# A third column block of w_down by the seven-product scheme, in a one-core decoder layer

## The chip, the cores and the metric

The kernel runs on one core of a Trainium2 chip. The metric is the device time of one execution in microseconds. TensorE (PE in the profile) multiplies, VectorE (DVE) and ScalarE (ACT) work on tiles element by element, GpSimd (POOL) and SyncE (SP) issue transfers between HBM and the on-chip memory SBUF. TensorE writes into eight accumulator banks (PSUM), each 128 partitions by 512 numbers of fp32.

## The reference

One decoder layer over 256 tokens plus 16 meta tokens, model width 2048, inner width 8192, everything in fp32. What matters here is its last part:

```python
u = rms_norm(h, g_pre_mlp[l])
f = jnp.square(jax.nn.relu(u @ w_up[l])) @ w_down[l]     # (256, 8192) @ (8192, 2048)
h = h + rms_norm(f, g_post_mlp[l])
```

Ahead of it stand a combined projection `u @ w_in`, a pooling branch, a convolution branch, and `m @ w_o`.

## The kernel before

**Precision.** Each fp32 matrix is split into a high part (a cast to fp32r on ScalarE) and a low part (the rest, a subtraction on VectorE), and a product is formed as high x high, high x low and low x high. A loaded block of weights is 1 MB, 128 partitions by 2048 numbers. It lies in a raw room; its two parts lie in rooms `hi0..hi2` and `lo0..lo2`, used in turn. So the parts of one product can only be written once the product three places earlier has been multiplied.

**Pieces.** The MLP runs over the inner width in NP = 8 pieces of PF = 1024. In each piece, `u @ w_up` makes 1024 columns (eight products U, named U h pair half: `U0a0` is half h = 0, pair a, first 1024 rows of w_up). Two products finish a pair of up tiles, which is summed out of the banks, scaled, put through relu and squared, and split into parts (`up_pair`, `relu_squared`). Then comes `f += s @ w_down` for that piece, with two token tiles t and two inner halves h of 512. The 2048 columns of w_down form four blocks n of 512 columns.

**Seven products.** Blocks 0 and 1 together are a 2 x 2 problem: token tiles by inner halves on one side, inner halves by column blocks on the other. The kernel solves it by Winograd's form of Strassen's scheme, with seven products P1 to P7 in place of eight. Each P multiplies one form of the activations (`A1`, `A2`: the plain tiles; `S1` to `S4`: sums and differences of them, held in `forms`) by one block of weights or a sum of blocks: `B11`, `B12`, `B21`, `B22`. The sums are made in the raw rooms by VectorE (`SUM_FOR`, 2.29 us planned each), for P5, P6, P7 and P4. `give` adds the finished bank to the result F in SBUF. Blocks 2 and 3 are multiplied plainly: X1 to X4, each one (h, n) for both token tiles, 24 matmuls of 512 columns, into the banks `x00, x01` (block 2) and `x10, x11` (block 3), which stay open over all pieces.

**Order.** A `Plan` collects the work with planned costs (2.72 us for 12 matmuls, 2.29 for a low part, 1.91 for a high part, a load 3.2 on SP plus 2.0 until it lands), the tiles read and written, and orders each engine by start times and due times that it works out from these. TensorE (PE) and SP keep the order in which the work was added; VectorE, ScalarE and GpSimd may be reordered when the program is built. Each engine then runs its own list in order. TensorE's order in a piece is in the strings `PIECE` and `NEXT`; a `+` marks a product of the next piece:

```python
PIECE = "U1a0 U1a1 P1 X1 U1b0 U1b1 X3"
NEXT = "U0a0+ P5 X2 P6 X4 P7 U0a1+ P3 U0b0+ P2 U0b1+ P4"
```

`weights(m)` adds sums and splits up to two products ahead. There are five raw rooms in the MLP (tiles a, c and three raw_m). `loads` hands a free room to the next block in `to_load`, and its transfer waits on SP until the room's last reader is through; SP issues in order. The bank `b` takes P5, P3 and P2 (`BANK`), bank `a` the others.

**Elsewhere.** In the w_o stage two blocks are added to a raw room by the transfer itself: `add_second` (line 1020) issues an adding transfer from GpSimd, planned with 1.0 + 9.0 us. Ahead of everything, the normed input u lies in one tile of 16 feature tiles.

Of the kernel before, what the change touches and what calls it, by code (L numbers as in the profile page):

```python
# [8 lines left out]
F32 = mybir.dt.float32  # L9
# [5 lines left out]
P = 128  # L15
# [6 lines left out]
class Plan:  # L22
# [29 lines left out]
    def order(self):  # L52
        n = len(self.work)
        after = [[] for _ in range(n)]
        for i, (_, _, _, before, _) in enumerate(self.work):
            for b in before:
                after[b].append(i)
        due, t = [float("inf")] * n, 0.0
        for i, (engine, cost, _, _, _) in enumerate(self.work):
            if engine == "PE":  # L60
                due[i] = t
                t += cost
        for i in reversed(range(n)):
            _, cost, _, _, late = self.work[i]
            for a in after[i]:
                due[i] = min(due[i], due[a] - cost - late - self.HOP)
        missing = [len(w[3]) for w in self.work]
        free_at = [0.0] * n
        clock = {w[0]: 0.0 for w in self.work}
        queue = {e: [i for i in range(n) if self.work[i][0] == e] for e in clock}  # L70
        start = [0.0] * n

        def begin(i):
            return max(clock[self.work[i][0]], free_at[i])
        for _ in range(n):
# [12 lines left out]
            queue[e].remove(best)  # L88
            for a in after[best]:
                free_at[a] = max(free_at[a], clock[e] + late + self.HOP)  # L90
                missing[a] -= 1
        self.start = start
        return sorted(range(n), key=lambda i: (start[i], i))

    def emit(self):
        for i in self.order():
            self.work[i][2]()


@with_exitstack  # L100
def hybrid_block(ctx: ExitStack, tc: tile.TileContext, ins: dict, out: bass.AP):
# [6 lines left out]
    NT = T // P  # L108
    KD = D // P
    w_in = ins["w_in"][0]  # L110
    w_grp = ins["w_pool_grp"][0]
# [271 lines left out]

    u = big.tile([P, KD, 2, -(-L // (4 * LINE)) * 4 * LINE], F32R, tag="um", name="u")[:, :, :, :L]

    def meta_tokens():
# [8 lines left out]
        nc.vector.tensor_mul(mg, pt, g[:, :, None].broadcast_to([P, KD, M]))  # L395
        nc.vector.tensor_copy(u[:, :, 0, :M], mg)
        return mg

    mg = meta_tokens()

    def low_of_meta():
        nc.vector.tensor_sub(u[:, :, 1, :M], mg, f32(u[:, :, 0, :M]))

# [173 lines left out]
    x_tile(0)  # L577
    low_of_meta()
    row(0)
# [5 lines left out]
    for k in range(KD):  # L585
# [3 lines left out]
        if k in (0, 2):  # L589
            for kx in (k + 2, k + 3):  # L590
                x_tile(kx)
                row(kx)
        elif k % 2 == 0 and k + 3 < KD:
            x_pair(k + 2)
        elif k + 3 < KD and k > 1:
            row(k + 3)
            row(k + 4)
        squares = {6: (0, 0), 8: (1, 0)}
        if k in squares:
# [753 lines left out]
    products = [s for s in steps if s[0] != "R"]  # L1353


    RAW_OF = {"P1": "B11", "P5": "B11", "P6": "B11", "P4": "B11", "P3": "B22", "P7": "B12",
              "P2": "B21"}
# [17 lines left out]
    for m_, (s, i) in enumerate(products):  # L1375
        if m_ >= len(opened):
            if s in SUM_FOR:
                uses.append((m_, "sum", [(r, i) for r in SUM_FOR[s]]))
            uses.append((m_, "split", [raw_of(s, i)]))
    last_use = {}  # L1380
    to_load = []
# [21 lines left out]
    for m_, (hi_, lo_, _, _) in enumerate(opened):  # L1403
        split_at[m_] = {"hi": hi_, "lo": lo_}

    def weights(m_):

        while uses and uses[0][0] <= m_:
            done = len(last_use_order) - len(uses)
            _, what, raws_ = uses.pop(0)  # L1410
            rooms = [room_at[r] for r in raws_]
            names = [f"raw{r}" for r in rooms]
            if what == "sum":
                a_, b_ = (room_of[r][:, :CK * CW] for r in rooms)
                plan.add("DVE", 2.29, lambda: nc.vector.tensor_add(a_, a_, b_),
                         reads=names, writes=names[:1])
            else:
                box = split_at[m_] = {}
                raw = room_of[rooms[0]][:, :CK * CW]
                n, q = first_n + m_, (first_n + m_) % 3  # L1420
                up = products[m_][0][0] == "U"
                rows = HALF[0] if up else CK

                def high():
                    box["flat"] = part_tile("hi", n, up)
                    nc.scalar.copy(box["flat"], raw)  # L1426
                    box["hi"] = box["flat"].rearrange("p (k c) -> p k c", k=rows)

                def low():
                    lo = part_tile("lo", n, up)  # L1430
                    nc.vector.tensor_sub(lo, raw, f32(box["flat"]))  # L1431
                    box["lo"] = lo.rearrange("p (k c) -> p k c", k=rows)
                plan.add("ACT", 1.91, high, reads=names, writes=(f"hi{q}",))
                plan.add("DVE", 2.29, low, reads=names + [f"hi{q}"], writes=(f"lo{q}",))
            for r in raws_:
# [64 lines left out]
    def relu_squared(h, pr, i, s_name, box):  # L1500
        ks = slice(2 * pr, 2 * pr + 2)
        G = forms[h]

# [13 lines left out]
        def q_(f):  # L1517
            return Q[:, f, ks, :]
        A = f"A{h}{pr}"
        plan.add("ACT", 0.75, square, reads=(s_name,), writes=(s_name,))  # L1520
# [5 lines left out]
        elif i < NP - 1:  # L1526
# [5 lines left out]
            plan.add("DVE", 0.42, lambda: nc.vector.tensor_add(q_(S4Q), a_(A1), q_(S2Q)),  # L1532
                     reads=(s_name, f"q3{pr}"), writes=(f"q4{pr}",))

        def dst(part):
# [25 lines left out]
    def up_done(h, pr, i, accs, acc_names):  # L1561
# [3 lines left out]
        else:  # L1565
            up_pair(h, pr, i, accs, acc_names, "s",
                    lambda: Q[:, SQ].rearrange("p k t -> p (k t)"))

# [19 lines left out]

    GIVES = {"P1": (0, 0, 1, True), "P2": (0, 0, 1, False), "P3": (0, 1, 1, False),
             "P4": (1, 0, 1, True), "P5": (1, 1, 1, True), "P6": (0, 1, -1, True),  # L1590
             "P7": (1, 1, -1, False)}


    def give(s, i):
        t, n, sign, first_ = GIVES[s]
        bank, dst, name = banks[BANK[s]], F[:, t, n, :], f"F{2 * t + n}"

        def f():
            if i == 0 and first_:
                nc.vector.tensor_scalar_mul(dst, bank, float(sign))  # L1600
# [21 lines left out]
    def product_plain(m_, s, i):  # L1622
        h, n = AT[s]
        for t, f in ((0, A1), (1, A2)):
            name = f"x{n - 2}{t}"
            plan.add("PE", 2.72, lambda t=t, f=f, name=name: down(
                banks[name], split_at[m_], h, f, i == 0 and h == 0,
                h == 1 and i == NP - 1 - (n == 3)),
# [17 lines left out]
    def product_block(m_, s, i):  # L1646
        h, f = FORM[s]
        plan.add("PE", 2.72, lambda: down(banks[BANK[s]], split_at[m_], h, f, s in OPENS, True),
                 reads=half_names(m_) + act_names(h, f), writes=(BANK[s],))
        give(s, i)  # L1650


# [27 lines left out]
    for s, i in steps:  # L1680
        if s == "R":
# [10 lines left out]
        {"U": product_up, "X": product_plain, "P": product_block, "Y": product_last}[s[0]](m_, s, i)  # L1692
        m_ += 1
# [40 lines left out]

    col_halves = [slice(h * HALF_CW, (h + 1) * HALF_CW) for h in range(2)]
    for e, cs in enumerate(col_halves):
# [88 lines left out]
```

## Time and profile before

| | us |
|---|---|
| median of 3 runs | 1206.31 (1206.03 to 1206.81) |
| profiled execution, its own time | 1206.4 |
| its span, first to last instruction | 1204.3 |
| TensorE busy | 1194.9 (99%) |
| VectorE busy | 974.5 (81%) |
| ScalarE busy | 624.3 (52%) |
| MLP pieces, from about 554 to the end | 84.4 each |

The profile records one execution. Matmuls overlap in their pipeline, so the time from one start to the next is what a matmul takes from the span, not the duration listed. In the lists of groups, the numbers behind the bar are the total busy time, the mean of one in nanoseconds, and the idle time of the engine just ahead of them with what ended it. The time to landing of a transfer is counted from its issue. In the view by stretches, each row gives the length, then for PE, PEld (weight loads), DVE, ACT and POOL the busy time and the number of instructions, then the granted clock of TensorE, the busy share of the DMA engines and GB/s.

### The profile page before, as it was taken

What the parts mean: (1) busy time and instruction counts of PE and PEld (TensorE: products, weight loads), DVE (VectorE), ACT (ScalarE), POOL (GpSimd) and SP (SyncE); (2) the same over time, 40 slices, a digit from 0 to 9 for tenths busy, and PEclk for the clock granted to TensorE, in tenths of its full rate; (3) what the DMA queues carried; (4) which work ended last, traced back from release to release, by engine and by line L of the source; (5) the groups of instructions that cost most, each with busy time, mean ns of one, the idle gap of its engine ahead of it and who ended that gap; (6) DMA issues with size and microseconds to landing.
All of it is one profiled execution on the core that took longest, in us unless ns stands there. A gap on an engine that the chain in (4) does not pass through costs nothing.

```text
span 1204.3 us, 15707 instructions
## 1 busy us (share of the span) xinstructions
PE 1194.9 (99%) x6442; PEld 1037.6 (86%) x6442; DVE 974.5 (81%) x1055; ACT 624.3 (52%) x633; POOL 8.8 (1%) x23
## 2 busy tenths in 40 slices
PE   9999999999999999999999999999999999999997
PEld 9999988888888888898888888888888888888886
DVE  6899978999676778688988878788878778788756
ACT  6533344443584455665555564564554555554543
POOL 1000000000000000000000000000000000000000
PEclk9999999999999999999999999999999999999999
DMA  9655555656558588546475665674764764755841
GB/s 290 210 177 183 187 189 185 200 186 199 183 167 285 169 267 262 169 168 217 146 239 175 192 227 163 196 250 139 244 199 157 261 198 151 245 175 173 276 146 70
DMA packets 162646, 238.27 MB, mean 198 GB/s; under 512 B 4145, under 2 KB 92401, under 8 KB 162064
## 3 DMA queue, kind: packets, MB, share of 16 engines
q1 hardware_dynamic: 160000, 230.64, 58.6%
q0 software_dynamic: 1680, 5.40, 1.7%
q10 hardware_dynamic: 896, 1.25, 0.3%
q8 instruction: 50, 0.82, 0.3%
q14 instruction: 20, 0.16, 0.0%
HBM read 235.17 MB, written 2.10 MB: 197 GB/s over the span
## 4 chain that ended last, share of the span: by engine, by line
PE 99%; DVE 1%; ACT 0%; DVEq 0%; ACTq 0%; issue 0%
PE bank_u L463 18%; PE acc_gate L746 14%; PE acc_up L1580 14%; PE bank_u L469 9%; PE bank_a L1580 7%; PE o_c L1084 6%; PE bank_b L1580 5%; PE acc_z L458 4%; PE acc_co L746 4%; PE acc_po L746 4%; PE acc_v L458 3%; PE acc_g L458 3%; PE acc_vg L458 2%; PE acc_up L463 1%; PE bank_u L1580 1%; PE o_a L1084 1%
## 5 line engine op out<-in xcount | busy, mean ns | idle before, releaser
L463 PE MATMUL bank_u<-m,hi 128*128 128x512 f32 x960 | 329.9, 390 | 0.0
L469 PE MATMUL bank_u<-m,lo 128*128 128x256 f32 x960 | 265.5, 277 | 0.0
L259 ACT CAST hi<-raw 128x2048 fp32r<-128x2048 f32 (+2 forms) x94 | 151.2, 1619 | 190.5 <-PE acc_gate L746 67.7
L1431 DVE TENSOR_TENSOR lo<-raw_m,hi 128x2048 fp32r<-128x2048 f32 x85 | 194.5, 2290 | 59.6 <-ACT hi L1426 59.5
L1426 ACT CAST hi<-raw_m 128x2048 fp32r<-128x2048 f32 x85 | 162.4, 1911 | 138.1 <-PE bank_u L463 76.8
L463 PEld LDWEIGHTS bank_u<-m,hi 128*128 128x128 f32 x960 | 180.2, 188 | 38.0
L262 DVE TENSOR_TENSOR lo<-raw,hi 128x2048 fp32r<-128x2048 f32 (+2 forms) x94 | 180.1, 1925 | 39.5 <-ACT hi L259 39.2
L469 PEld LDWEIGHTS bank_u<-m,lo 128*128 128x128 f32 x960 | 180.3, 188 | 1.6
L746 PE MATMUL acc_gate<-hi,u 128*128 128x512 f32 x512 | 158.4, 390 | 0.0
L1580 PE MATMUL acc_up<-hi,forms 128*128 128x512 f32 x496 | 157.5, 389 | 0.0
L524 DVE SCALAR_TENSOR_TENSOR c<-a,taps,c 128x256 f32<-128x256 f32 x240 | 115.7, 484 | 6.8
L746 PEld LDWEIGHTS acc_gate<-hi,u 128*128 128x128 f32 x512 | 96.1, 188 | 19.9
L1580 PEld LDWEIGHTS acc_up<-hi,forms 128*128 128x128 f32 x496 | 93.1, 188 | 19.5
L746 PE MATMUL acc_gate<-lo,u 128*128 128x512 f32 x256 | 99.6, 389 | 0.0
L1580 PE MATMUL acc_up<-lo,forms 128*128 128x512 f32 x248 | 96.6, 389 | 0.0
L1431 DVE TENSOR_TENSOR lo<-raw_c,hi 128x2048 fp32r<-128x2048 f32 x29 | 66.4, 2290 | 21.2 <-ACT hi L1426 21.2
L1580 PE MATMUL bank_a<-hi,forms 128*128 128x512 f32 (+1 forms) x256 | 82.0, 383 | 0.0
L1426 ACT CAST hi<-raw_c 128x2048 fp32r<-128x2048 f32 x29 | 55.3, 1908 | 51.0 <-PE bank_u L463 27.9
L1431 DVE TENSOR_TENSOR lo<-raw_a,hi 128x2048 fp32r<-128x2048 f32 x29 | 66.4, 2290 | 17.5 <-ACT hi L1426 17.5
L1426 ACT CAST hi<-raw_a 128x2048 fp32r<-128x2048 f32 x29 | 55.4, 1910 | 42.4 <-PE bank_u L463 19.4
L1084 PE MATMUL o_c<-hi,m 128*128 128x512 f32 x208 | 65.6, 390 | 0.0
L1580 PE MATMUL bank_b<-hi,forms 128*128 128x512 f32 (+1 forms) x200 | 63.7, 382 | 0.0
(327 smaller groups left out, 1850.8 us busy)
## 6 DMA issues: line engine op xcount, KB each, us to landing
raw<-in_w_in_dram SPq DMA_DIRECT2D x52, 1024.0 KB, 5.2
raw_m<-in_w_down_dram SPq DMA_DIRECT2D x37, 1024.0 KB, 5.2
raw_m<-in_w_up_dram SPq DMA_DIRECT2D x33, 1024.0 KB, 6.4
raw_c<-in_w_down_dram SPq DMA_DIRECT2D x14, 1024.0 KB, 5.1
raw_a<-in_w_up_dram SPq DMA_DIRECT2D x13, 1024.0 KB, 6.0
raw_a<-in_w_down_dram SPq DMA_DIRECT2D x13, 1024.0 KB, 5.3
raw_c<-in_w_up_dram SPq DMA_DIRECT2D x12, 1024.0 KB, 5.8
raw_o<-in_w_o_dram SPq DMA_DIRECT2D x10, 1024.0 KB, 7.4
```

The costliest lines, as they stand in the source:

```text
L259: nc.scalar.copy(hi[:, sl, cs], raw[:, sl, cs])
L262: nc.vector.tensor_sub(lo[:, sl, cs], raw[:, sl, cs], f32(hi[:, sl, cs]))
L458: nc.tensor.matmul(acc, w[:, k[0], cs], act[:, k[1], a, off:], start=first and n == 0, stop=last and n == 2)
L463: nc.tensor.matmul(acc.rearrange("p (a t) -> p a t", a=2)[:, :, ts], hi[:, k[0], cs], act[:, k[1], :, off + ts.start:off + ts.stop], start ...
L469: nc.tensor.matmul(acc[:, :T], lo[:, k[0], cs], act[:, k[1], 0, off:], start=False, stop=stop, skip_group_check=True)
L524: nc.vector.scalar_tensor_tensor(c, conv["a"][:, q, i:i + T], taps[:, q, i:i + 1], c, op0=ALU.mult, op1=ALU.add)
L746: nc.tensor.matmul(acc, act(kk)[:, a_, ts_], w_[:, k, :], start=kk == 0 and n == 0, stop=kk == nk - 1 and n == 2)
L1084: nc.tensor.matmul(acc, form(k, a_), box[w_][:, k, :], start=start and k == 0 and n == 0, stop=stop and k == CK - 1 and n == 2, skip_group ...
L1426: nc.scalar.copy(box["flat"], raw)
L1431: nc.vector.tensor_sub(lo, raw, f32(box["flat"]))
L1580: nc.tensor.matmul(acc, forms[h][:, f, k, a_, :], box[w_][:, k, cs], start=start and k == 0 and n == 0, stop=stop and k == KH - 1 and n == ...
```

## The change

Block 2 of w_down is now computed by the same seven-product scheme, its two column halves of 256 taking the place of the two column blocks. X1 and X2 stay the names of its two loaded blocks (h = 0 and 1). Where a piece multiplied X1 and X2 (two 512-column products each), it now multiplies E1 to E5, seven products of 12 matmuls with 256 columns. E1 has P1 and P5 of the scheme side by side in bank `b`, E2 has P2 and P3 in `x00`, E3 puts P6 onto P1 in bank `b`, E4 puts P4 into `x01`, E5 puts P7 onto P1 + P6. After E1, E3 and E5 ScalarE copies the bank out (`save_e`) and VectorE adds or subtracts it into `x00` and `x01` (`add_e`). The sums of weights T1 to T4 are made on half-width columns in the raw rooms (`sum_e`). E4 needs only half a block split, and E5 reads E3's parts again. The last piece keeps X1 and X2.

The sums for P5 (B11 + B12) and P7 (B12 + B22) are no longer made by VectorE: GpSimd issues an adding transfer of the second block onto the room that holds the first (`BRINGS`). For P5 this follows P1's split; for P7 it stands six products ahead, and B12 is loaded for it.

The order of products in a piece is new, the sums of the up tiles' pairs lie in four rooms in place of one (three of them in the tile `pairs`), and the parts of the next piece's activations are written after the last product that reads the old ones (`deferred`). The tile u is two tiles, of 13 and 3 feature tiles, so that `pairs` can take the place of the second one. The bank x01 is set to zero ahead of the pieces. The planner no longer counts a hop between two operations of one engine.

```diff
-                free_at[a] = max(free_at[a], clock[e] + late + self.HOP)
+                hop = self.HOP if self.work[a][0] != e else 0.0
+                free_at[a] = max(free_at[a], clock[e] + late + hop)
...
+    BRING_AHEAD = 6
...
-    u = big.tile([P, KD, 2, -(-L // (4 * LINE)) * 4 * LINE], F32R, tag="um", name="u")[:, :, :, :L]
+    u = Tiles([big.tile([P, n, 2, -(-L // (4 * LINE)) * 4 * LINE], F32R, tag=tag,
+                        name=f"u_{tag}")[:, :, :, :L] for tag, n in (("um", KM), ("ux", KD - KM))], KM)
...
+    pairs_room = big.tile([P, 3, 2 * T], F32, tag="ux", name="pairs")
...
-    FIRST_PIECE = "U1a0 U1a1 U1b0 R U1b1 P1 X1 X3"
-    PIECE = "U1a0 U1a1 P1 X1 U1b0 U1b1 X3"
-    NEXT = "U0a0+ P5 X2 P6 X4 P7 U0a1+ P3 U0b0+ P2 U0b1+ P4"
-    LAST_PIECE = "U1a0 U1a1 Y1 U1b0 U1b1 X1 Y3 Y2 Y4 X2 X3 X4"
+    FIRST_PIECE = "U1a0 U1a1 U1b0 R U1b1 P1 X3 X4"
+    PIECE = "U1b1 P1 X3 X4"
+    NEXT = "U0a0+ E2 E1 U0a1+ E3 E4 E5 U0b0+ P5 U0b1+ P3 P6 U1a0+ P7 U1a1+ P2 P4 U1b0+"
+    LAST_PIECE = "Y1 U1b1 X1 Y3 Y2 Y4 X2 X3 X4"
...
-    SUM_FOR = {"P5": ("B11", "B12"), "P6": ("B11", "B22"), "P7": ("B12", "B22"),
-               "P4": ("B11", "B21")}
+               "P2": "B21", "E1": "X1", "E2": "X2", "E3": "X1", "E4": "X2"}
+    SUM_FOR = {"P6": ("B11", "B22"), "P4": ("B11", "B21")}
+    BRINGS = {"P1": ("B11", "B12", 0), "P7": ("B12", "B22", BRING_AHEAD)}
+    SUMS_E = {"E1": ["T1"], "E3": ["T2", "T4", "T3"]}
...
+            if s in BRINGS:
+                to, what, ahead = BRINGS[s]
+                uses.append((m_ - ahead, "bring " + what, [(to, i)]))
+    uses.sort(key=lambda use: use[0])
...
+        f, dst, a_, b_, wrote = {"T1": (nc.vector.tensor_add, b12, b12, b11, 0),
+                                 "T2": (nc.vector.tensor_add, b12, b12, b22, 0),
+                                 "T4": (nc.vector.tensor_add, b21, b12, b21, 1),
+                                 "T3": (nc.vector.tensor_sub, b11, b12, b11, 0)}[what]
+        plan.add("DVE", 1.22, lambda: f(dst, a_, b_), reads=names, writes=names[wrote:wrote + 1])
...
+            elif what[:5] == "bring":
+                src, (rows, _) = source(what[6:], raws_[0][1])
+                plan.add("POOL", 1.0, lambda src=src, dst=room_of[rooms[0]][:, :CK * CW].rearrange(
+                    "p (k c) -> p k c", k=rows): nc.gpsimd.dma_start(dst, src, accum_op=ALU.add),
+                    reads=names, writes=names, late=9.0)
...
+    def times_e(m_, h, f, bank, half, start, name):
+        cs = col_halves[half[0]]
+        plan.add("PE", 1.36, lambda: [
+            nc.tensor.matmul(banks[bank][:, col_halves[half[1]]], forms[h][:, f, k, a_, :],
+                             split_at[m_][w_][:, k, cs], start=start and k == 0 and n == 0,
+                             stop=False, skip_group_check=True)
+            for k in range(KH) for n, (a_, w_) in enumerate(((0, "hi"), (0, "lo"), (1, "hi")))],
+            reads=half_names(m_) + act_names(h, f), writes=(bank,) + (name,) * (name != bank))
+
+    def save_e(key, cs, cost):
+        def f():
+            box_e[key] = st = tmp.tile([P, CW], F32, tag="junk", bufs=1, name=f"st_{key}")[:, cs] \
+                if key == "E1" else tmp.tile([P, T], F32, tag="v", bufs=5, name=f"st_{key}")
+            nc.scalar.copy(st, banks["b"][:, cs])
+        plan.add("ACT", cost, f, reads=("b",), writes=("st" + key,))
...
+        if s == "E2":
+            for n, f in enumerate((A1, S4)):
+                times_e(m_, 1, f, "x00", (n, n), i == 0 and n == 0, "x00")
+        elif s == "E1":
+            for n, f in enumerate((A1, S1)):
+                times_e(m_, 0, f, "b", (n, n), n == 0, "b")
+            save_e("E1", all_, 0.62)
+            add_e("E1", all_, 0, all_, 1)
+            add_e("E1", h1_, 1, h1_, 1)
+        elif s == "E3":
+            times_e(m_, 1, S2, "b", (1, 0), False, "b")
+            save_e("E3", h0, 0.37)
+            add_e("E3", slice(0, T), 0, h1_, -1)
+        elif s == "E4":
+            times_e(m_, 1, A2, "x01", (0, 0), False, "x01")
+        else:
+            times_e(m_, 0, S3, "b", (0, 0), False, "b")
+            save_e("E5", h0, 0.37)
+            add_e("E5", slice(0, T), 1, h0, 1)
+            add_e("E5", slice(0, T), 1, h1_, -1)
...
+    plan.add("DVE", 0.5, lambda: nc.vector.memset(banks["x01"], 0.0), writes=("x01",))
...
+        if s == "E5":
+            product_e(e3_at, s, i)
+            continue
-        for w in range(m_, min(m_ + 3, len(products))):
+        for w in range(m_, min(m_ + (2 if s == "E4" else 3), len(products))):
```

More of the change, by code (lines that the diff above doesn't have):

```diff
@@ L97, in emit, with __init__, __getitem__ @@
             self.work[i][2]()
+class Tiles:
+    def __init__(self, rooms, n):
+        self.rooms, self.n, self.shape = rooms, n, rooms[0].shape
+    def __getitem__(self, at):
+        p, k, *rest = at
+        return self.rooms[k >= self.n][(p, k - self.n * (k >= self.n), *rest)]
 @with_exitstack
@@ L109, in hybrid_block @@
     KD = D // P
+    KM = 13
     w_in = ins["w_in"][0]
@@ L1378, in hybrid_block @@
                 uses.append((m_, "sum", [(r, i) for r in SUM_FOR[s]]))
+            for what in SUMS_E.get(s, ()):
+                uses.append((m_, what, [("X1", i)] + [("X2", i)] * (s == "E3")))
             uses.append((m_, "split", [raw_of(s, i)]))
+            if s in BRINGS:
+                to, what, ahead = BRINGS[s]
+                uses.append((m_ - ahead, "bring " + what, [(to, i)]))
+    uses.sort(key=lambda use: use[0])
     last_use = {}
@@ L1409, in weights @@
             done = len(last_use_order) - len(uses)
-            _, what, raws_ = uses.pop(0)
+            at_, what, raws_ = uses.pop(0)
             rooms = [room_at[r] for r in raws_]
@@ L1413, in weights @@
             if what == "sum":
-                a_, b_ = (room_of[r][:, :CK * CW] for r in rooms)
-                plan.add("DVE", 2.29, lambda: nc.vector.tensor_add(a_, a_, b_),
+                plan.add("DVE", 2.29, lambda a_=room_of[rooms[0]][:, :CK * CW],
+                         b_=room_of[rooms[1]][:, :CK * CW]: nc.vector.tensor_add(a_, a_, b_),
                          reads=names, writes=names[:1])
-            else:
[L1418 to L1434, printed above, removed]
+            elif what[:5] == "bring":
[3 more added lines that the diff above has]
+                    reads=names, writes=names, late=9.0)
+            elif what[0] == "T":
+                sum_e(what, rooms, names)
+            else:
+                split_raw(at_, rooms[0], names)
             for r in raws_:
```

100 lines of the change are left out of this document (81 added, 19 removed).

## The prediction

> **What bounds the kernel now.** I read the page first, then the busy time by stretches, then single rows.
>
> ```profile
> span 1204.3 us, 15707 instructions
> PE 1194.9 (99%) x6442; PEld 1037.6 (86%) x6442; DVE 974.5 (81%) x1055; ACT 624.3 (52%) x633; POOL 8.8 (1%) x23
> PE 99%; DVE 1%; ACT 0%; DVEq 0%; ACTq 0%; issue 0%
> ```
>
> The chain that ended last is matmuls for 99% of the span, so the time is the sum of the spacings of the matmuls plus every gap opened between them. In the MLP, two of its eight pieces look like this in the view by stretches (last columns: granted clock, DMA share, GB/s):
>
> ```profile
> 707.40:791.80 84.40, 84.40 (x437) 72.24 (x437) 68.87 (x59) 46.03 (x41) 0.00 (x0) 1.00 0.62 200
> 791.80:876.20 84.40, 84.40 (x437) 72.22 (x436) 68.86 (x59) 46.03 (x41) 0.00 (x0) 1.00 0.61 198
> ```
>
> A piece takes 84.40 us and TensorE never rests; VectorE works 68.9 us of it and ScalarE 46.0, so both have room. A matmul's listed duration is not its price, since they overlap: the price is the distance between starts. The timeline of TensorE gives it:
>
> ```profile
> 699.59 0.39 PE L463 MATMUL bank_u<-m,hi 128*128 128x512 f32 x1
> 699.82 0.28 PE L469 MATMUL bank_u<-m,lo 128*128 128x256 f32 x1
> 699.93 0.39 PE L463 MATMUL bank_u<-m,hi 128*128 128x512 f32 x1
> ...
> 1187.21 0.62 PE L1580 MATMUL acc_up<-hi,forms 128*128 128x512 f32 x2
> 1187.66 0.39 PE L1580 MATMUL acc_up<-lo,forms 128*128 128x512 f32 x1
> 1187.89 0.62 PE L1580 MATMUL acc_up<-hi,forms 128*128 128x512 f32 x2
> ...
> 1190.15 0.28 PE L1580 MATMUL bank_a<-hi,forms 128*128 128x256 f32 x1
> ...
> 1192.91 0.28 PE L1580 MATMUL bank_a<-hi,forms 128*128 128x256 f32 x1
> ```
>
> Three 512-column matmuls take 1187.89 - 1187.21 = 0.68, so 0.227 us each. The 24 matmuls of 256 columns into bank_a, the same form that the change uses, have 23 spacings in 2.76 us: 0.120 each, a little over half. An up pair (512, then 256) takes 0.34, so an up product of 16 pairs takes 5.46 with the small loss at its edges; a P product of 12 takes 2.72.
>
> **Part 1, the matmuls.** Each of the first seven pieces loses X1 and X2, 48 matmuls of 512 columns (48 x 0.227 = 10.88 us), and gains E1 to E5, 2 + 2 + 1 + 1 + 1 = 7 products of 12 matmuls of 256 columns (84 x 0.120 = 10.08). That is 0.80 us a piece, 5.6 in all. It lies on the path and comes off the span whole, if no gap opens.
>
> **Part 2, VectorE and ScalarE.**
>
> ```profile
> L1431 DVE TENSOR_TENSOR lo<-raw_m,hi 128x2048 fp32r<-128x2048 f32 x85 | 194.5, 2290 | 59.6 <-ACT hi L1426 59.5
> L1426 ACT CAST hi<-raw_m 128x2048 fp32r<-128x2048 f32 x85 | 162.4, 1911 | 138.1 <-PE bank_u L463 76.8 <-PE acc_up L1580 25.5 <-issue 14.4
> L1557 DVE TENSOR_TENSOR forms<-F_raw,forms 128x512 fp32r<-128x512 f32 x28 | 19.2, 686 | 0.0
> L1487 DVE TENSOR_TENSOR F_raw<-half,bank_u 128x256 f32<-128x256 f32 x60 | 25.0, 417 | 10.7 <-ACT half L1480 9.9
> L1480 ACT COPY half<-bank_u 128x256 f32<-128x256 f32 x60 | 22.2, 369 | 35.6 <-PE bank_u L469 35.6
> ```
>
> VectorE gets, a piece: one more low part (2.29) and half of one (1.24, midway between rows), the four half-wide sums T1 to T4 (1024 elements; no row has that size, between 0.69 for 512 and 2.29 for 2048; I take 1.22 on the line between), and the adds into the banks (0.69 + 4 x 0.42). That is 10.8 us; the two sums that become transfers take off 2 x 2.29. Net +6.2: 75 of 83.6 us. ScalarE gets 1.91 + 1.05 + 0.62 + 2 x 0.37 = 4.3, so 50. Totals fit, so this costs nothing by itself. What counts is the distance between a product and the third one after it, because there are three rooms for split parts. Before, the tightest distance was P plus X, 8.2 us. Now U0b0 has only E3, E4 and E5 between, 36 x 0.120 = 4.32, to get its split done. What the split needs is in these rows:
>
> ```profile
> 704.69 0.40 PE L1580 MATMUL bank_a<-hi,forms 128*128 128x512 f32 x1
> 704.78 1.91 ACT L1426 CAST hi<-raw_c 128x2048 fp32r<-128x2048 f32 x1 [2.23 <-PE bank_u L463]
> 706.59 0.36 ACT L1480 COPY half<-bank_u 128x256 f32<-128x256 f32 x1
> 706.71 2.29 DVE L1431 TENSOR_TENSOR lo<-raw_c,hi 128x2048 fp32r<-128x2048 f32 x1 [1.27 <-ACT hi L1426]
> ```
>
> The high part starts 0.09 after the product that frees its room (the next begins at 704.69), the low part 0.02 after the high: 0.09 + 1.91 + 0.02 + 2.29 = 4.31. It just fits; I charge 0.
>
> **Part 3, the adding transfers.** The trace has two of them, in the w_o stage. This is the second, and the plain load issued behind it; below that a plain load of w_up in the MLP with nothing beside it:
>
> ```profile
> L1023 POOL DMA_DIRECT2D raw<-in_w_o_dram x1: 1277/1277/1277, 455.2 to 455.2; - x1
> ...
> DMA to landing us min/median/max: 10.0/10.0/10.0
> ```
>
> ```profile
> L1016 SPq DMA_DIRECT2D raw_o<-in_w_o_dram x1: 368/368/368, 456.9 to 456.9; - x1
> ...
> DMA to landing us min/median/max: 9.5/9.5/9.5
> ```
>
> ```profile
> L1393 SPq DMA_DIRECT2D raw_m<-in_w_up_dram x1: 368/368/368, 717.2 to 717.2; - x1
> ...
> DMA to landing us min/median/max: 5.7/5.7/5.7
> ```
>
> The adding transfer took 10.0 us, and the plain load issued 1.7 us behind it took 9.5 in place of some 5.2 to 5.7. The planner books 10 us for the one and 5.2 for the other always; it knows nothing of the slowing. So I walk the stretch where this falls, with 0 at the start of U0a1 (TensorE: U0a1 0, E3 5.46, E4 6.90, E5 8.34, U0b0 9.78, P5 15.24, U0b1 17.96).
>
> U0a1's own parts: room free when U0a0 ends, at -5.76; high to -3.76, low to -1.4. Its raw room is empty then, and SP issues the load of B12 into it. That lands 5.2 later, at 3.8, and POOL at once issues B22 on top (bring B12 += B22 for P7). E3: ScalarE does E4's half from 0.09 to 1.1, E3's high part to 3.0, VectorE E3's low part to 5.3, in time for 5.46. This empties the room that U0b1's load waits for on SP: issued at 5.35, 1.5 us behind the adding transfer, nearly the case of the row. Behind U0b1 on SP stands only B22's load, needed by P3 and P6 later. Alone, U0b1's load lands at 11.05; at 9.5 us it lands at 14.85.
>
> In the built order ScalarE runs P5's high part (9.87 to 11.78), then U0b1's, and then the copy of bank b behind E5; P5 overwrites bank b and waits for that copy. ScalarE is in order, so it stands before U0b1's high part until the load lands: high part 14.9 to 16.8, copy (starting 0.09 before the listed end, as at 706.59) to 17.1, P5 at 17.15 and not 15.24. That is a gap of 1.9 us on TensorE. U0b1's low part ends at 19.1, before P5 does (19.87), so no second gap. The seven pieces with E steps all have this order: 7 x 1.9 = 13.3.
>
> The bounds of this term: a load may take 15.24 - 5.35 - 1.91 - 0.37 - 0.1 = 7.5 us without a gap. Below it the cost is 0, and no gain. From above: a load in the w_o stage issued behind an adding and a broadcast transfer took longer still.
>
> ```profile
> L1016 SPq DMA_DIRECT2D raw_o<-in_w_o_dram x1: 367/367/367, 439.0 to 439.0; - x1
> ...
> DMA to landing us min/median/max: 12.4/12.4/12.4
> ```
>
> 12.4 us would cost 4.8 a piece, 34 in all. I take 9.5, one transfer against one with nearly the same lead. [...]
>
> The other adding transfer (B11 += B12, issued behind P1's split, some 6.7 us ahead of U1b1's end) has some 40 us until P5; the load beside it is X1's, wanted first by T1 with 2 to 3 us in hand. I charge 0; without that cover each us late is at most one us of gap, 7 in all. POOL is idle in the pieces (0.00 above), so its 1.28 us of issuing queues nothing.
>
> **Part 4, the rest.** The split of u into two rooms adds two small VectorE operations, the bank's memset one (0.5 us planned), behind matmuls; four pair rooms only loosen waits. 0, within 0.3 either way.
>
> **Sum**, against the profiled execution's own time of 1206.4, of which 2.1 lie outside the span and stay (the median of the runs is 1206.31, 0.1 less): 1206.4 - 5.6 + 13.3 - 0.1 = 1214.0 us.
>
> **Rivals.**
> (a) The load is not slowed enough to matter: U0b1 lands within 7.5 us. For it: 1.8 us of reserve over a lone load, and B12 landing 2 us later than walked would let U0b1's packets go first. Against it: the 9.5. It gives 1206.3 - 5.6 = 1200.7. [...]
> (b) In between, 8.0 to 8.6 us: a gap of 0.5 to 1.1, 3.5 to 7.7 in all, so 1204 to 1208.5, no change.
> (c) VectorE is late at E3. It decides from T sums of about 1.9 us on: at 2.29 each, T2, T4 and T3 push U0a1's low part past its start by 0.4 and E3's to 0.9 to 1.3 late; 7 x 1 on top of (a) is 1208. Against it: every two-operand row scales with its elements.
> (d) The scheme isn't worth its matmuls. It breaks even at 10.88/84 = 0.1295 us; 23 spacings say 0.120. Hardly open.
>
> **How the numbers follow.** Forecast 0.48, (a) 0.34, (b) 0.12, (c) and (d) 0.06. Slower by over 0.2% (2.4 us, about what can be told from no change) takes the forecast and (c), (d): 0.54; same 0.12; faster 0.34. The forecast's own range, loads of 8.7 to 10.3 us, is 1209 to 1219; since (a) is too likely to leave out, the whole range is 1200 to 1219.
>
> **What would show it.** Right: TensorE idle some 2 us ahead of each P5, seven times, released by ScalarE's copy of bank b, behind a high part that a w_up load released; that load at 9 to 10 us; E matmuls 0.12 apart. Wrong: no gaps at P5 (then a), gaps at E3 or U0b0 ended by VectorE (then c), or a load that starts its packets before the adding transfer's.

## The result, and the profile after

The changed kernel takes 1240.5 us (median of 5 runs, 1240.49 to 1242.54) against 1206.2 for the one before: a ratio of 1.0289, interval 1.0274 to 1.0304. The forecast was 1214.0 with a range of 1200 to 1219, so the direction was right and the time lies far outside the range. The profiled execution's span is 1238.8 us, 34.5 more than before.

From the page of the changed kernel: the span, the busy times, the row of the granted clock in 40 slices, the chain of waits, and the one group of matmuls with a large idle time ahead of it.

```profile
span 1238.8 us, 16346 instructions
PE 1206.0 (97%) x6694; PEld 1055.5 (85%) x6694; DVE 1016.2 (82%) x1121; ACT 649.5 (52%) x668; POOL 26.7 (2%) x37
PEclk9999999999999999999899999999899999998999
PE 91%; DMA 7%; ACT 1%; DVE 0%; SPq 0%; issue 0%; DVEq 0%; ACTq 0%
L1660 PE MATMUL bank_b<-hi,forms 128*128 128x512 f32 (+1 forms) x200 | 72.9, 431 | 23.3 <-ACT st_E L1751 23.3
```

Before, the chain that ended last was 99% matmuls; now 7% of it is transfers. The idle time stands ahead of matmuls into bank b, and what ended it is the copy of that bank, `st_E`, as the prediction said. But the same matmuls also show a mean of 431 ns, and the clock row has 8s in it, where that of the kernel before has 9s alone. The same group before:

```profile
L1580 PE MATMUL bank_b<-hi,forms 128*128 128x512 f32 (+1 forms) x200 | 63.7, 382 | 0.0
```

The adding transfer and U0b1's load in one piece, by source line (duration of the issue in ns, its time, and then the time to landing):

```profile
L1488 POOL DMA_DIRECT2D raw_m<-in_w_down_dram x1: 1277/1277/1277, 680.9 to 680.9; - x1
...
DMA to landing us min/median/max: 10.3/10.3/10.3
```

```profile
L1429 SPq DMA_DIRECT2D raw_c<-in_w_up_dram x1: 368/368/368, 682.0 to 682.0; - x1
...
  ACT hi L1466: 4.3, 1
...
DMA to landing us min/median/max: 10.8/10.8/10.8
```

The timelines of ScalarE and of TensorE around the gap that follows (start, duration, engine, line, operation, and in brackets the idle time before it):

```profile
686.71 1.91 ACT L1466 CAST hi<-raw_m 128x2048 fp32r<-128x2048 f32 x1 [1.95 <-PE bank_b L1741]
692.89 1.90 ACT L1466 CAST hi<-raw_c 128x2048 fp32r<-128x2048 f32 x1 [4.27 <-DMA raw_c<-in_w_up_dram]
694.70 0.37 ACT L1751 COPY st_E<-bank_b 128x256 f32<-128x256 f32 x1
```

```profile
691.85 0.28 PE L489 MATMUL bank_u<-m,lo 128*128 128x256 f32 x1
695.12 0.61 PE L1660 MATMUL bank_b<-hi,forms 128*128 128x512 f32 x1 [2.99 <-ACT st_E L1751]
695.53 0.63 PE L1660 MATMUL bank_b<-lo,forms 128*128 128x512 f32 x1
695.95 1.05 PE L1660 MATMUL bank_b<-hi,forms 128*128 128x512 f32 x2
```

This is the walked chain, step for step: the load of U0b1 lands at 692.9, ScalarE has sat idle 4.27 us with the copy of bank b behind the high part in its list, the copy follows at 694.70, and P5 starts at 695.12. P5 was due 0.12 after the last matmul of U0b0, at 691.97. So the gap is 3.15 us, where 1.9 was forecast.

What was not forecast is in the lines after it. The 512-column matmuls start at 695.12, 695.53 and 695.95, some 0.42 us apart in place of 0.227. The view by stretches around two of the seven gaps shows why (the last three numbers are granted clock, DMA share, GB/s):

```profile
694.00:700.00 6.00, 4.88 (x15) 3.88 (x16) 5.17 (x3) 4.55 (x7) 0.00 (x0) 0.72 0.83 264
...
1051.00:1054.00 3.00, 1.90 (x8) 1.60 (x9) 2.19 (x1) 2.97 (x6) 0.00 (x0) 1.00 1.08 368
```

After the 3.15 us gap the granted clock over the stretch is 0.72 (0.50 for 3.41 us of it, by the record of the clock); after the shortest gap, 2.46 us at 1052.10, it stays at 1.00. From the starts of all matmuls, gap by gap (the last column is what the matmuls behind the gap start further apart than at full clock, summed):

| P5 starts at | U0b1's load, us | gap, us | lost to slow matmuls after it, us |
|---|---|---|---|
| 605.9 | 12.8 | 4.97 | 2.05 |
| 695.1 | 10.8 | 3.15 | 1.71 |
| 784.0 | 10.8 | 3.12 | 1.69 |
| 873.4 | 11.4 | 3.55 | 3.01 |
| 963.6 | 11.0 | 3.18 | 1.71 |
| 1052.1 | 10.3 | 2.46 | 0.11 |
| 1140.1 | 11.7 | 4.01 | 2.82 |
| sum | | 24.4 | 13.1 |

The two sums make 37.5 us; the span grew by 34.5, so the rest of the change saved 3.0.

### The profile page after: what moved, and what is told of

It is laid out like the page before. It is cut to its first block, busy times and chain, and to the rows that moved or that the text cites. A ratio compares the mean times of both kernels' runs of the same rounds, so it can differ in the third digit from the quotient of the medians.

```text
span 1238.8 us, 16346 instructions
## 1 busy us (share of the span) xinstructions
PE 1206.0 (97%) x6694; PEld 1055.5 (85%) x6694; DVE 1016.2 (82%) x1121; ACT 649.5 (52%) x668; POOL 26.7 (2%) x37
## 4 chain that ended last, share of the span: by engine, by line
PE 91%; DMA 7%; ACT 1%; DVE 0%; SPq 0%; issue 0%; DVEq 0%; ACTq 0%
PE bank_u L483 16%; PE acc_gate L769 14%; PE bank_u L489 8%; PE acc_up L1660 7%; PE bank_a L1660 7%; PE bank_b L1660 6%; PE o_c L1108 6%; DMA raw_m<-in_w_up_dram 5%; PE acc_z L478 4%; PE acc_co L769 4%; PE acc_po L769 4%; PE acc_v L478 3%; PE acc_g L478 3%; PE acc_vg L478 2%; DMA raw_c<-in_w_up_dram 2%; PE bank_b L1741 2%
## 5 line engine op out<-in xcount | busy, mean ns | idle before, releaser
L1466 ACT CAST hi<-raw_m 128x2048 fp32r<-128x2048 f32 (+1 forms) x94 | 175.0, 1865 | 159.1 <-PE bank_u L483 31.6
L1470 DVE TENSOR_TENSOR lo<-raw_m,hi 128x2048 fp32r<-128x2048 f32 (+1 forms) x94 | 209.9, 2234 | 53.7 <-ACT hi L1466 53.2
L769 PE MATMUL acc_gate<-hi,u_um 128*128 128x512 f32 x416 | 131.5, 390 | 0.0
L769 PEld LDWEIGHTS acc_gate<-hi,u_um 128*128 128x128 f32 x416 | 78.1, 188 | 16.3
L1466 ACT CAST hi<-raw_c 128x2048 fp32r<-128x2048 f32 (+1 forms) x33 | 61.2, 1854 | 57.5 <-PE bank_b L1741 11.8
L1470 DVE TENSOR_TENSOR lo<-raw_c,hi 128x2048 fp32r<-128x2048 f32 (+1 forms) x33 | 73.5, 2226 | 20.8 <-ACT hi L1466 20.7
L1660 PE MATMUL acc_up<-hi,forms 128*128 128x512 f32 x272 | 85.2, 389 | 0.0
L769 PE MATMUL acc_gate<-lo,u_um 128*128 128x512 f32 x208 | 80.9, 389 | 0.0
L1660 PEld LDWEIGHTS bank_b<-hi,forms 128*128 128x128 f32 x200 | 42.3, 214 | 34.9 <-ACT st_E L1751 25.5
L1660 PEld LDWEIGHTS acc_up<-hi,forms 128*128 128x128 f32 x272 | 51.1, 188 | 10.6
```

The source lines that it names most:

```text
L769: nc.tensor.matmul(acc, act(kk)[:, a_, ts_], w_[:, k, :], start=kk == 0 and n == 0, stop=kk == nk - 1 and n == 2)
L1466: nc.scalar.copy(box["hi"][:, :, cs], raw)
L1470: nc.vector.tensor_sub(box["lo"][:, :, cs], raw, f32(box["hi"][:, :, cs]))
L1660: nc.tensor.matmul(acc, forms[h][:, f, k, a_, :], box[w_][:, k, cs], start=start and k == 0 and n == 0, stop=stop and k == KH - 1 and n == ...
```

## The experiments

Four questions stood open: whether the adding transfer is the whole cause, what the E scheme is worth without it, why the load took longer than 9.5 us, and what the slow matmuls come from. The kernel before, run on the same chips, took 1205.6 to 1206.4. Where no number of runs is given, the time is that of one run.

**The adding transfer moved: `BRING_AHEAD`.** It stands four products ahead of P7 in place of six.

```
-    BRING_AHEAD = 6
+    BRING_AHEAD = 4
```

> BRING_AHEAD 4 in place of 6: B12's load now stands behind U0b1's on SP, so U0b1's load is issued before the adding transfer B12 += B22 exists. Theory A (the adding transfer slows U0b1's load, ScalarE stands before U0b1's high part, the copy of bank b and with it P5 wait; the clock falls after the gap): U0b1's load takes 5 to 6 us, no gap at P5, clock back to 1.00, 1200 to 1203 us. Rival B (the E steps themselves make ScalarE or VectorE late at P5): gaps of 2.5 to 5 us stay, 1235 to 1245.

Measured: 1234.87 us (5 runs, 1231.27 to 1235.95), ratio 1.0231 (1.0218 to 1.0245). The gaps at P5 went, and six came up inside U1a0, between its first two matmuls, of 1.1 to 4.4 us, 19.8 in all. The timelines of TensorE and VectorE in one piece:

```profile
703.77 0.40 PE L483 MATMUL bank_u<-m,hi 128*128 128x512 f32 x1
707.43 0.39 PE L489 MATMUL bank_u<-m,lo 128*128 128x256 f32 x1 [3.26 <-DVE lo L1470]
```

```profile
702.88 2.29 DVE L1483 TENSOR_TENSOR raw_m<-raw_m,raw_m 128x2048 f32<-128x2048 f32 x1 [3.17 <-DMA raw_m<-in_w_down_dram]
705.09 2.29 DVE L1470 TENSOR_TENSOR lo<-raw_a,hi 128x2048 fp32r<-128x2048 f32 x1
```

The same pattern on another engine: VectorE, in order, stands at a sum whose block is late, and U1a0's low part stands behind it. The adding transfer of this piece took 13.9 us. Of the two loads behind it, the one issued 0.3 us later took 7.0 us and landed first, and the one issued 3.3 us later took 12.5. Moving the transfer moved the wait; it did not find a place with nothing behind it.

**P7's sum by VectorE again.** P5's adding transfer stays.

```
-    SUM_FOR = {"P6": ("B11", "B22"), "P4": ("B11", "B21")}
+    SUM_FOR = {"P6": ("B11", "B22"), "P7": ("B12", "B22"), "P4": ("B11", "B21")}
-    BRINGS = {"P1": ("B11", "B12", 0), "P7": ("B12", "B22", BRING_AHEAD)}
+    BRINGS = {"P1": ("B11", "B12", 0)}
```

> The sum for P7 made by VectorE again, the other transfer (B11 += B12) kept. Theory A: no adding transfer is in flight at U0b1's load, no gap at P5; VectorE has 2.3 us more a piece, 1200 to 1206 us. Rival B: unchanged or worse, 1238 to 1255, since VectorE works more. Rival D (the first adding transfer is to blame): unchanged, about 1240.

Measured: 1202.8 us. No gap over 0.1 us is left in the MLP. U0b1's load in one piece, and the span and chain of waits:

```profile
L1429 SPq DMA_DIRECT2D raw_m<-in_w_up_dram x1: 368/368/368, 667.2 to 667.2; - x1
...
DMA to landing us min/median/max: 6.0/6.0/6.0
```

```profile
span 1200.8 us, 16332 instructions
PE 99%; DVE 0%; DVEq 0%; ACT 0%; issue 0%; ACTq 0%
```

So P7's transfer alone costs 38 us of span, and it only took 2.29 us a piece off an engine with room. Two things went with it: the adding, and B12's early load. The room that B12's load took now goes to U0b1's load, which is issued 16.9 us ahead of P5 in place of 9.9. P5's transfer, charged at 0, opens no gap. The same kernel, timed in more runs:

> The kernel of e2_p7_sum again, timed in rounds against the kernel before, since one look gave 1202.8: theory A 1202 to 1204 us, ratio 0.996 to 0.998; if the one look was luck, 1206 or more.

Measured: 1202.62 us (1202.07 to 1203.04), ratio 0.9969 (0.9957 to 0.9981). This version beats both kernels, the one before by 0.3%.

**Both sums by VectorE**, `BRINGS` empty and P5 and P7 in `SUM_FOR`.

> Both sums made by VectorE, no adding transfer in the pieces at all; the E steps and the new order stay. Theory A: no gap at P5 by a load; VectorE has 4.6 us a piece more than the changed kernel, some 79 of 84 us. If that still fits, 1202 to 1204 us, and the transfers bring nothing; if VectorE now binds, gaps ended by VectorE, 1206 to 1220.

Measured: 1208.87 us (11 runs, 1207.41 to 1209.79), ratio 1.0021 (1.0012 to 1.003). Seven gaps of 0.63 to 0.64 us (4.4 in all) ahead of U0b0, and 1.8 us of small ones. TensorE and VectorE there:

```profile
678.89 0.28 PE L1741 MATMUL bank_b<-hi,forms 128*128 128x256 f32 x1
679.65 0.50 PE L483 MATMUL bank_u<-m,hi 128*128 128x512 f32 x1 [0.47 <-DVE F_raw L1546]
```

```profile
674.77 2.28 DVE L1483 TENSOR_TENSOR raw_m<-raw_m,raw_m 128x2048 f32<-128x2048 f32 x1
676.97 2.28 DVE L1470 TENSOR_TENSOR lo<-raw_c,hi 128x2048 fp32r<-128x2048 f32 x1
679.17 0.75 DVE L1546 TENSOR_TENSOR F_raw<-half,bank_u 128x256 f32<-128x256 f32 x2
```

A full sum, at 674.77, stands in VectorE's list with two other operations back to back behind it, and the reading of bank u comes late. P5's transfer is thus worth its place: 6.2 us between the medians, which is about those gaps.

This run also has U0b1's load where the changed kernel has it, with B22's load 0.4 us behind it, and no adding transfer near. In the seven pieces it takes 8.0 to 8.6 us; in one:

```profile
L1429 SPq DMA_DIRECT2D raw_a<-in_w_up_dram x1: 368/368/368, 674.6 to 674.6; - x1
...
DMA to landing us min/median/max: 8.6/8.6/8.6
```

So a load at this place is not the lone load of 5.7 us, even without an adding transfer. ScalarE waits 1.97 us for it here, and P5, behind a late U0b0, still starts 0.16 us late.

**P5's sum by VectorE, P7's transfer kept.** As P7's transfer now stands ahead of P5's sum, the sum B11 + B12 that P5 multiplies has B22 in it too.

```
-    SUM_FOR = {"P6": ("B11", "B22"), "P4": ("B11", "B21")}
+    SUM_FOR = {"P5": ("B11", "B12"), "P6": ("B11", "B22"), "P4": ("B11", "B21")}
-    BRINGS = {"P1": ("B11", "B12", 0), "P7": ("B12", "B22", BRING_AHEAD)}
+    BRINGS = {"P7": ("B12", "B22", BRING_AHEAD)}
```

> The other half undone: the sum for P5 by VectorE, the adding transfer for P7 kept. Theory A: the gaps at P5 stay, 2.5 to 5 us each with slow matmuls behind them, 1232 to 1246 us. Rival (it takes both transfers): 1201 to 1210 us.

Measured: 1285.25 us, with gaps of 5.5 to 9.9 us at P5, and 2.25 after its first matmul. P5's own split now waits, through the sum, for the transfer itself: in one piece it lands at 701.1, the sum (2.29) and the high part (1.9) bring that to 705.3, and P5 starts at 705.38. That is a new dependence and not the old one doubled, so the run doesn't answer what it was made for.

**The planner told the truth** about U0b1's load.

```
-            writes=(f"raw{room}",), late=2.0)
+            writes=(f"raw{room}",), late=7.6 if r[0] == "U0b1" else 2.0)
```

> The planner is told that U0b1's load lands 7.6 us behind its 3.2 on SP, so ScalarE's list has the copy of bank b ahead of U0b1's high part; transfers stay. Theory A: P5 starts on time, the load stays at 10 to 13 us, and the wait moves to U0b1 itself, 1.5 to 3.5 us in place of 2.5 to 5: 1212 to 1228 us. Rival (the copy's place in ScalarE's list is of no account): gaps at P5 as before, about 1240.

Measured: 1209.51 us. The wait did not move to U0b1. E3's sums and split were put earlier instead, so that the room came free sooner and U0b1's load went out 3.0 us ahead of the adding transfer, not behind it:

```profile
L1429 SPq DMA_DIRECT2D raw_c<-in_w_up_dram x1: 367/367/367, 672.4 to 672.4; - x1
...
DMA to landing us min/median/max: 6.1/6.1/6.1
```

There is no gap at P5. Six of 0.94 us and one of 0.97 are inside E1, whose activations come late on VectorE behind the three sums and the low part that were put forward. Two things changed at once: the order of the two transfers, and the place of the copy of bank b, which now stands ahead of U0b1's high part (683.47 and 683.73 in this piece). By the walk's limit of 7.5 us a load of 6.1 leaves no gap whichever way the copy stands. The run is 31 us shorter than that of the changed kernel.

**The adding transfers as plain copies**, of the same bytes into the same rooms at the same places; the sums B11 + B12 and B12 + B22 are left out.

```
-                    nc.gpsimd.dma_start(dst, src, accum_op=ALU.add),
+                    nc.gpsimd.dma_start(dst, src),
```

> Both transfers from GpSimd stay, at the same places and of the same size, but as plain copies: the sums B11 + B12 and B12 + B22 are left out, the room then holds the second block alone. Theory A with the adding to blame: the copy is over in about half the time, U0b1's load takes 7 to 9 us, gaps of 0 to 1.5 us and no slow clock, 1201 to 1212. Rival C (any 1 MB beside the loads does it, the adding is of no account): U0b1's load 10 to 13 us, 1235 to 1245.

Measured: 1208.62 us. The copies land in 5.5 to 5.7 us in place of 9.8 to 13.7, U0b1's load behind them in 8.2 to 9.0; the gaps at P5 are 0.46 to 1.26 us, 5.8 in all, and no matmuls are slow. The load of the piece shown above:

```profile
L1429 SPq DMA_DIRECT2D raw_c<-in_w_up_dram x1: 368/368/368, 675.7 to 675.7; - x1
...
DMA to landing us min/median/max: 8.4/8.4/8.4
```

With no transfer from GpSimd near, the load at this place takes 8.3 us on average (the run with both sums by VectorE); with a plain transfer of 1 MB in front it takes 8.6, and with the adding one 11.3. So the adding transfer costs the load some 3 us, and a plain copy of the same size 0.3. Of the 38 us that P7's transfer costs, 32 go with the adding.

**Larger packets.** U0b1's load is made in rows of 512 numbers (2 KB) in place of 256, as w_down's are; other weights are thereby multiplied in that block.

```
+            if what == "U0b1":
+                return columns(w_up, c * HALF[0], CK, i * PF + h * CW)[0]
```

> The changed kernel, with U0b1's load as 4 by 512 columns in place of 8 by 256, so in packets of 2 KB and not 1 KB, as the load of the w_o stage had that took 9.5 us beside an adding transfer. The wrong weights stand in that block, so that part of the output is left out. Theory (packets of the two queues take turns, and a load of 1 KB packets gets half the rate): the load takes 9.0 to 9.8 us, gaps of 1.2 to 2.0 us, clock at 1.00, 1211 to 1219 us. Rival (the size of packets is of no account): 10.3 to 12.8 us, about 1240 us.

Measured: 1233.39 us, the load in 10.3 to 11.4 us, the adding transfers in 10.8 to 13.9, gaps 2.5 to 3.7. The size of the load's packets is not why it took more than 9.5 us: the load gained about half a microsecond on average, and the adding transfer lost 1.4. With packets of 1 KB, in the changed kernel from 684 to 690 us, the queue with the adding transfer moved 451 packets and 0.91 MB, and that with U0b1's load 405 packets and 0.41 MB.

**The load behind it.** B22's load, 0.4 us behind U0b1's, brings one of its four rows in six of the pieces; the other three rows are left out, and P3 and P6 multiply old contents there.

```
+        if r[0] == "B22" and 0 < r[1] < NP - 1:
+            src, dst = src[:, :1], dst[:, :1]
```

> In six of the seven pieces (not the first) the load of B22 that stands 0.4 us behind U0b1's load on SP's queue brings only the first of its four rows, a quarter of its bytes; the other three rows of that weight block are left out, so P3 and P6 multiply old contents there. The first piece is left as it is. If U0b1's load takes 10.3 to 12.8 us and not 9.5 because B22's load shares the engines with it and with the adding transfer: it lands within 8.5 to 9.8 us in those six pieces, the gap ahead of P5 falls from 2.5 to 4.0 to 1.0 to 2.2 us and the slow stretches behind it mostly go; about 1219 to 1226 us. If the adding transfer alone sets it: still 10.3 us or more, gaps of 2.5 and more, 1235 to 1241 us. In both the first piece keeps a gap of about 5 us.

Measured: 1240.04 us, gaps of 2.8 to 4.5 us in the six pieces, the load in 10.5 to 12.2. Both loads of one piece, the full one and the quarter:

```profile
L1432 SPq DMA_DIRECT2D raw_c<-in_w_up_dram x1: 367/367/367, 681.1 to 681.1; - x1
L1432 SPq DMA_DIRECT2D raw_m<-in_w_down_dram x1: 599/599/599, 681.5 to 681.5; - x1
...
DMA to landing us min/median/max: 10.6/10.7/10.8
```

So, with the adding transfer in flight, what stands behind U0b1's load did not matter to it here: 10.5 to 12.2 us against 10.3 to 11.7 in the same six pieces of the changed kernel. The quarter's 10.8 us say nothing of size, for it stands behind U0b1's full load on the same queue and lands 0.7 us after it, where the whole block in the changed kernel lands 2.7 us after it. In the six pieces U0b1's load, issued 0.9 to 1.3 us behind the adding transfer, lands 0.5 to 2.0 us after that one.

**Gaps of a chosen length with no adding transfer there.** In the kernel without P7's transfer, ScalarE copies bank b out 18, 24 and 13 times after E5 (24 and 13 with the same line).

```
-            nc.scalar.copy(st, banks["b"][:, cs])
+            for _ in range(18 if key == "E5" else 1):
+                nc.scalar.copy(st, banks["b"][:, cs])
```

> On the kernel of e2_p7_sum (no gap there): ScalarE makes its copy of bank b behind E5 18 times in place of once, some 0.28 us each, so P5 waits by about 2 us without any transfer. Theory of the clock (a gap over some 2.5 us halves TensorE's clock for some 4 us, whatever made the gap): gap under the limit, matmuls behind it at 0.227, only the gap counts: 1202.8 + 7 x 2 = 1217 us. Rival (slow matmuls come from transfers beside them): the same here.

> The same with 24 copies, a gap of some 3.8 us in each of seven pieces. Theory of the clock: matmuls behind the gap at twice their spacing for some 4 us, 1.9 us more a piece: 1202.8 + 7 x 5.7 = 1243 us. Rival (slow matmuls come from transfers beside them): no slow matmuls, 1202.8 + 7 x 3.8 = 1229 us.

> On the kernel of e2_p7_sum, 13 copies of bank b: by 18 and 24 copies (gaps of 4.0 and 6.6 us, 0.43 a copy) a gap of 1.9 us. Theory of the clock (it falls only behind a gap longer than one between 2.5 and 3.0 us): no slow matmuls, 1202.6 + 7 x 1.9 = 1216 us. Rival (any gap of a microsecond or two makes the clock fall): 2.1 us more a piece, 1230 us.

Measured: 1247.34, 1262.45 and 1223.17 us; a further copy costs some 0.43 us, so the gaps are longer than meant: 4.0 to 4.2, 6.5 to 6.7, and 2.05 to 2.21 us. After each gap of the first two the matmuls lose 1.6 to 2.9 us, with little on the DMA queues: in this stretch of the 18 copies the clock is 0.52 at a DMA share of 0.15.

```profile
693.00:700.00 7.00, 5.51 (x13) 4.36 (x14) 2.24 (x1) 4.60 (x8) 0.00 (x0) 0.52 0.15 51
```

So the clock fell behind gaps that copies made (0.52 here) as behind those that a transfer made (0.72 in the stretch shown first), and in these runs the gap is what the two have in common. With 13 copies it falls after three of seven gaps that are all but equal, so the threshold expected between 2.5 and 3.0 us is not there. The 4 us after the first two:

```profile
602.60:606.60 4.00, 3.96 (x19) 3.32 (x20) 0.89 (x2) 3.97 (x5) 0.00 (x0) 1.00 0.38 131
688.90:692.90 4.00, 4.00 (x11) 3.14 (x12) 0.90 (x2) 3.16 (x4) 0.00 (x0) 0.59 0.33 108
```

19 matmuls or 11 in the same 4 us, after gaps of 2.17 and 2.21. TensorE counts as busy either way; only the count and the clock tell.

The record of the granted clock tells which gaps count. In all eight runs with gaps of 2 us or more the clock stands at 0.50 for 3.41 us, or for two or three times that, and within a run these stretches begin whole multiples of 3.41 us apart. (The ends of the executions, where TensorE is done, are left out here and below.) So the time can be cut into slices of 3.41 us on that grid. Three slices of this run, with gaps of 2.21, 2.06 and 2.20 us, each with the slice behind it:

```profile
686.20:689.61 3.41, 1.36 (x7) 0.95 (x6) 2.79 (x2) 3.19 (x9) 0.00 (x0) 1.00 1.05 366
689.61:693.02 3.41, 3.41 (x9) 2.65 (x9) 0.89 (x1) 2.49 (x3) 0.00 (x0) 0.50 0.17 55
...
860.28:863.69 3.41, 1.51 (x9) 1.02 (x7) 2.73 (x2) 3.19 (x9) 0.00 (x0) 1.00 1.04 349
863.69:867.10 3.41, 3.41 (x10) 2.63 (x9) 0.94 (x1) 2.43 (x3) 0.00 (x0) 0.50 0.18 61
...
949.03:952.44 3.41, 1.61 (x7) 1.35 (x8) 1.97 (x1) 3.25 (x9) 0.00 (x0) 1.00 0.94 308
952.44:955.85 3.41, 3.41 (x20) 2.94 (x19) 1.74 (x1) 3.41 (x2) 0.00 (x0) 1.00 0.02 6
```

The first two gaps lie within one slice, which leaves TensorE 1.36 and 1.51 us of work in it, and the next slice is at half clock. The third lies across the edge of two, 1.61 us of work are left in the slice, and the clock stays. All eight runs agree: the clock fell behind each of the 47 slices at full clock in which TensorE was idle for 1.90 us or more (the length less the busy time), and behind none with 1.81 or less. In the changed kernel these were six slices with 2.05 to 2.99 us idle, and the largest without a fall had 1.76. At half clock, a slice with up to 0.59 us idle was the last, and one with 0.60 or more was followed by another. So here the place of a gap on the grid decided, as well as its length: the clock fell behind the gap of 2.06 us and not behind the one of 2.20.

## Why the prediction was off

**Part 1, right in sign, 2.1 us too large.** In the kernel without P7's transfer, where nothing else is in the way, P5 comes every 83.9 to 84.1 us, against 84.56 before. These are the two stretches from P5 to P5 (before, then without P7's transfer):

```profile
663.77:748.33 84.56, 84.56 (x439) 72.44 (x437) 69.02 (x59) 46.03 (x41) 0.00 (x0) 1.00 0.62 199
```

```profile
684.19:768.24 84.05, 84.05 (x474) 73.65 (x473) 76.90 (x69) 49.63 (x46) 1.26 (x1) 1.00 0.67 214
```

That is 0.5 us a piece and not 0.80. (The prediction's stretches of 84.40 were a little shorter than a piece.) By the spans (1204.3 and 1200.8) 3.5 of the 5.6 came. By the starts of all matmuls in the MLP, the E products are not to blame: their 588 matmuls run at 0.120 us apart, as taken. The up products of both kernels are the same, yet they took some 1.9 us longer in all; why, no run here tells.

**Part 2, right.** VectorE works 74.9 us of a piece in the changed kernel (75 forecast) and ScalarE 49.7 (50), by the stretch from P5 to P5:

```profile
695.12:783.99 88.87, 85.91 (x472) 74.79 (x472) 74.87 (x68) 49.71 (x47) 2.54 (x2) 0.98 0.71 212
```

No gap opened at U0b0 or E3; the one thing that did not fit was a second full sum, as the run with both sums on VectorE shows. Part 4, put at 0, holds too: the MLP's first matmul starts at 511.8 us, against 511.5 before.

**Part 3, the mechanism right, its price too low.** This is the step that failed, in two terms. Counted as in the walk, with U0a1 starting 15.24 before P5 was due (at 676.73), B12's load was issued at -1.5 (forecast -1.4) and landed at 3.6 (3.8), the adding transfer went out at 4.2 (3.8), U0b1's load at 5.3 (5.35); only its landing, at 16.1 (14.85), was off.

The first term is the load: "I take 9.5" rested on one row of one execution. The same load stands behind the same adding transfer at the same lead of 1.7 us in the w_o stage of every kernel here, and in the changed one it took

```profile
L1040 SPq DMA_DIRECT2D raw_o<-in_w_o_dram x1: 367/367/367, 457.3 to 457.3; - x1
...
DMA to landing us min/median/max: 10.8/10.8/10.8
```

In the profiles of the twelve experiments it took 9.7 once and 10.6 to 11.0 otherwise. The 9.5 was the lowest of fourteen. With 10.8 the walk gives 1.9 + 1.3 = 3.2 a gap and 22.4 in all, near the 24.4 measured; the rest is the first and last such pieces, where the adding transfer took 13.7 and 11.0. The upper bound, 12.4 us and 34 in all, did hold for all but one load (12.8), but the prediction did not take it into its range.

The walk also compared with the wrong load. "Alone, U0b1's load lands at 11.05" takes the row of a lone load, 5.7 us, but B22's load stands 0.4 us behind this one. With that neighbour and no adding transfer it takes 8.0 to 8.6 us, over the limit of 7.5 by itself. With the adding transfer in flight, B22's load made no difference, so this step did not add to the miss.

The second term was missing. Seven gaps were priced at their length, but six of them also cost 1.7 to 3.0 us of matmuls at a lower clock: 13.1 us that no step of the prediction had. With the measured terms, Part 1's as well, the sum is 1206.4 - 3.5 + 24.4 + 13.1 = 1240.4.

**The rivals.** (a) needed the load within 7.5 us, and none was under 10.3; at this place it was not open even without the adding transfer, as the 8.0 us show. Its time of 1200.7 is, but for Part 1, that of the kernel without P7's transfer, 1202.6. (c) did not show in the changed kernel: the T sums take 1.22 us, as assumed. It shows in the kernel with the truthful plan, where those sums stand earlier in VectorE's list. (d) is out at 0.120.

**What stays open.** Why an adding transfer of 1 MB took about twice a plain one's time here (9.8 to 13.7 us against 5.5 to 5.7 at the same place), no run tells. The one of 13.7 us in the first piece goes with a short lead: U0b1's load was issued 0.70 us behind it there, and 0.97 to 1.29 behind the others. In the run with `BRING_AHEAD = 4`, adding transfers with a load 0.3 to 0.7 us behind them took 13.5 to 14.8 us, and the one with 1.36 took 9.1. The mechanism behind this stays open.

## What to carry to other kernels

Price a wait on TensorE at more than its length: in these runs gaps of 2.05 us and more had up to 3.0 us of slow matmuls behind them (1.7 behind one of 3.15), while those of up to 1.3 us cost only themselves. By that, one long gap cost more here than several short ones of the same sum: seven of 2.46 to 4.97 us, 24.4 in all, had 13.1 us behind them, and seven of 0.46 to 1.26, 5.8 in all, had none. A load of 1 MB issued about a microsecond behind an adding transfer landed about when that one was through: in the changed kernel, at 0.7 to 1.3 us behind, 0.1 us before it to 2.4 after. The case is no wider than that: loads issued 0.3 to 0.7 us behind one, in the run with `BRING_AHEAD = 4`, landed 1.6 to 6.9 us before it. A time taken from one row of contention carries a spread that belongs in the range, and the lone load to compare with is one with the same neighbours. The adding transfer paid where it relieved an engine that had no room and had nothing urgent behind it (P5's, 6.2 us), and not where the engine had the 2.3 us anyway (P7's, which cost 38).

## What the runs showed of the hardware

In the eight runs with gaps of 2 us or more, the granted clock stood at 0.50 behind each slice of 3.41 us, on a grid that is fixed within a run, in which TensorE was idle for 1.90 us or more, and behind none with 1.81 or less. So no gap up to 1.3 us had it, of those of 2.05 to 2.5 us some had it and some not, and above 2.6 us all but one (2.77 us in the run with the short load, split into 0.97 and 1.81 by the grid). The slow stretch lasted 3.41 us or a whole multiple of it (3.41 three times and 6.83 three times in the changed kernel), and cost 1.4 to 3.0 us, mostly some 1.7. Half of 3.41 us would be 1.7, an estimate from the measured length and clock that agrees with the commonest loss.

An adding transfer of 1 MB took 8.3 to 14.8 us in these runs' MLP (8.4 to 13.7 in the changed kernel), and a plain one from GpSimd 5.4 to 7.4.
